# One more block of gates by seven products ahead of attention, and a new distribution of the filling work over the forgetting heads

## The chip, the cores and the metric

The kernel runs on one core of one Trainium2 chip. The core has five engines that run side by side, each through its own list of instructions in order: TensorE (PE) for matrix products, VectorE (DVE), ScalarE (ACT), GpSimd (POOL) and SyncE (SP), which mostly issues DMAs. The metric is the time of one execution on the device, in microseconds (us). Where several executions are given, their median counts.

## The reference, cut to what matters

The layer works on x of 1024 rows by 1024 columns in float32. It is a half feed-forward, then two attentions side by side with gates, then a second half feed-forward and a gated embedding. The middle part is what the change touches:

```python
h = rms_norm(x, mix_norm[i])
fq, fk, fv, f_logit, sq, sk, sv, g_fox, g_sb = split_columns(h @ w_in[i])
fq = rms_norm(fq.reshape(b, s_len, FOX_HEADS, HEAD_DIM), q_norm[i])
fk = rms_norm(fk.reshape(b, s_len, FOX_HEADS, HEAD_DIM), k_norm[i])
log_f = jax.nn.log_sigmoid((f_logit + forget_bias[i]).astype(jnp.float32))
y_fox = forgetting_attention(fq, fk, fv, log_f)
y_sb = stick_breaking_attention(sq, sk, sv)
merged = (jax.nn.sigmoid(g_fox) * (y_fox @ w_branch_fox[i])
          + jax.nn.sigmoid(g_sb) * (y_sb @ w_branch_sb[i]))
x = x + merged @ w_out[i]
```

There are eight forgetting heads (softmax with an added forget term) and eight stick-breaking heads, each 64 wide. The gates g_fox and g_sb are 2048 columns of `h @ w_in`, each passed through a sigmoid. Nothing needs them before the merge, so they may be computed at any time between the norm and the merge.

## The kernel before, in words

Every float32 product is made of three passes over operands that are split into a high part (a rounded copy, by ACT) and a low part (the remainder, by DVE or POOL): high x high, high x low, low x high. A product of 128 gate columns with 512 rows thus takes 3 passes of 8 matmuls, 24 in all, and 48 for all 1024 rows (`g_units`, L915, whose matmuls are at L807).

The gates come in 16 tiles of 128 columns. The first twelve are made ahead of attention by `make_up` (matmuls at L556) in `NG = 6` blocks of 256 columns. A block is a 2 by 2 by 2 product of halves, which `make_up` makes with seven products of 12 matmuls each instead of eight, after sums and differences of the operand blocks have been formed; block 0 alone is made plainly (L506). `up_order` writes out the order of the products, and preparing of weight pieces (`prep`) runs four products ahead. The list `hl` names the buffer for each prepared piece. The order in this stage is the program's.

The last four gate tiles (12 to 15) are made inside attention as filling. `attention` (L1260 on) goes through 16 heads, forgetting heads 0 to 7 and then stick-breaking heads 8 to 15, each in four steps c = 0 to 3 of two blocks of rows. A step emits `scores` of its two row blocks (matmuls at L1050 and L1051) and, two steps late, `apply` (transposes at L1109, copies at L1111 and L1117, value matmuls at L1135). Between these, `take` draws instructions from the head's list in `fill`, at a pace given by the list's total cost, spread over 7, 8, 5 and 6 calls of the four steps (shares 0.27, 0.19, 0.27, 0.27). The first call of a head comes right after the score matmuls of its row block 0, and the last call of a head precedes four value matmuls. The list of a head is used up before the next head begins. All matmuls and transposes go through `pe`, which ties them to the order of emission, so TensorE cannot swap a filling matmul with another one. The order of the other engines inside the forgetting heads is left to a planner that works before the run.

The filling units are:

- `fox_qk_units` (eight units a pair of heads): 24 matmuls of 256 columns each (L799) make q and k of 128 rows. ACT squares and copies them (L863, L864), DVE sums (L865). At t = 3 and t = 7, DVE (L868), POOL with a power (L869) and POOL with a multiplication (L871) norm the half that has just been completed.
- `v_units` (eight units): 24 matmuls of 256 columns each (L799).
- `fox_stack_units` (two halves a head): four transposes of a normed half (L897), then ACT, DVE and four DMAs (L884, L885, L887) put the head's q and k into stacks for the scores. The first half feeds row blocks 0 to 3, the second half row blocks 4 to 7. A half is entered with a cost of 0.436 and a pause of 1.5 that holds no TensorE work.
- `sb_stack_units` and `g_units` (two halves each): 24 matmuls of 512 columns (L807) a half. A gate half ends with a sigmoid on ACT (L926).

Two halves of the filling's weights are split at a time from `RAW` into `WH` (ACT, L129) and `WL` (POOL, L139). There are three buffers of each, so a new cell's weights wait for the buffers of the cell before.

Of the kernel before, what the change touches and what calls it, by code (L numbers as in the profile page):

```python
# [36 lines left out]
def tile_hybrid_decoder_layer(  # L37
# [794 lines left out]
    def v_units(col, extra, cell, new_bank=fill_bank):  # L832
        n = 256 + extra
        add_load(cell, lambda: mix_nat([(col, col + n)], NAT))

        def unit(t):
            weights(cell)
            if t == 0:
                cell["v"] = slot("X", [P, NT, 4, P], F32R)
            ps = new_bank()  # L840
            yield from nat_steps(ps, t, cell["w"], n, hT)
            v2 = cell["v"]
            src = ps[:, :256].rearrange("p (h d) -> p h d", h=4)
            split(v2[:, t, :, 0:HD], v2[:, t, :, HD:P], src, nc.scalar, nc.vector)
            if extra:
                nc.vector.tensor_copy(lfs[:, t, :], ps[:, 256:264])
        return [(24 * 0.109, unit(t)) for t in range(NT)]

    def fox_qk_units(pair, cell, tags=NAT, sq_tag="PT", new_bank=fill_bank):
        add_load(cell, lambda: mix_nat([(FQ + pair * P, FQ + pair * P + P), (FK + pair * P, FK + pair * P + P)], tags))  # L850

        def unit(t):
            weights(cell)
            if t == 0:
                cell["n"] = [slot("RN", [P, 4, 2, 2, HD]) for _ in range(2)]
                cell["ss"] = [stat([P, 4, 4], "qkss", 4) for _ in range(2)]
            half, q = divmod(t, 4)
            ps = new_bank()
            yield from nat_steps(ps, t, cell["w"], 256, hT)
            N = cell["n"][half]  # L860
            src = ps[:, :256].rearrange("p (s h d) -> p s h d", s=2, h=2)
            sq = slot(sq_tag, [P, 256])
            nc.scalar.activation(sq[:].rearrange("p (h s d) -> p s h d", s=2, h=2), src, AF.Square)  # L863
            nc.scalar.copy(N[:, q].rearrange("p h s d -> p s h d"), src)  # L864
            nc.vector.reduce_sum(cell["ss"][half][:, q, :], sq[:].rearrange("p (g d) -> p g d", g=4), axis=AX.X)  # L865
            if q == 3:
                ss = cell["ss"][half][:].rearrange("p a b -> p (a b)")
                nc.vector.tensor_scalar(ss, ss, 1.0 / HD, EPS, ALU.mult, ALU.add)  # L868
                nc.gpsimd.tensor_tensor(ss, ss, mhalf[:], ALU.pow)  # L869
                nv = N[:].rearrange("p a h s d -> p (a h s) d")  # L870
                nc.gpsimd.tensor_mul(nv, nv, ss.unsqueeze(2).broadcast_to([P, 16, HD]))  # L871
        return [(24 * 0.109, unit(t)) for t in range(NT)]
# [44 lines left out]
    def g_units(m, new_bank=fill_bank):  # L917
        cell = {}

        add_load(cell, lambda: wload([kp(win)[:, :, GFOX + m * P:GFOX + m * P + P]], KD, P))  # L920

        def unit(half):
            ps = new_bank()
            yield from feat_steps(ps, half, weights(cell))
            g = slot("PT", [P, 512])
            order("act", nc.scalar.activation(g[:], ps[:], AF.Sigmoid))  # L926
            nc.sync.dma_start(gd[m, :, half * 512:half * 512 + 512], g[:])
        return [(24 * 0.216, unit(0)), (24 * 0.216, unit(1))]
# [250 lines left out]
    FOX_PAIRS = [2, 3, 0, 1]  # L1179
    mx = {}  # L1180

    NG = 6

    def mix_start():

        mx["v"], mx["qk"] = {}, {}
        mx["u1"] = v_units(FV + 256, NH, mx["v"], wide_bank)
        tags = (("T", "Y"), ("T", "Y"))
        mx["u2"] = fox_qk_units(FOX_PAIRS[0], mx["qk"], tags, "KH", wide_bank)
        q0 = FOX_PAIRS[0] * P  # L1190
        pieces = [[kp(win)[:, 4 * kh:4 * kh + 4, a:a + n] for a, n in cols] for cols in (((FV + 256, 256 + NH),), ((FQ + q0, P), (FK + q0, P))) for kh in range(2)]
        raws = {}
        N, Xs = [], []

        def gate_out(n, i, e):
            nc.sync.dma_start(gd[2 * n + i].rearrange("p (h n) -> p h n", h=2), e[:])

        def load_qk(i):
            if i == 0:
                raws["qk"] = [wraw_load(pieces[2 + kh], 4, 256, ("KH", "KL")[kh]) for kh in range(2)]  # L1200
        cycle = ("WL", "WL", "WL", "Q", "Q", "PT")
        hl = ["WL", "WL", "WL", "KL"] + ["PT"] * 4 + ["WL", "WL", "WL", "PT"]
        hl += [cycle[k % 6] for k in range(12, 7 * NG - 6)] + ["WL", "WH", "WH", "Q"]
        tags_g = {"raw": UP_TAGS["raw"], "sum": UP_TAGS["sum"], "w": UP_TAGS["w"], "hl": hl, "t1": "X",
                  "B": {"12": "H", 3: "H", 5: ("Y", "Y", "T", "T"), 6: ("T",) * 4, 7: "X", 4: "X"}}
        F = make_up(N, lambda n: kp(win)[:, :, GFOX + n * 256:GFOX + n * 256 + 256], NG, tags_g, AF.Sigmoid, gate_out, load_qk)
        E = F.E

        def evict(n, m, ps):
            if m == 1:  # L1210
                E[n] = [slot(t, [P, 2, 512]) for t in ("GF", "RN")]
            e1, e2 = E[n]
            if m == 1:
                nc.scalar.copy(e1[:, 0, :], ps[:])
            elif m == 6:
                nc.scalar.copy(e1[:, 1, :], ps[:])
            elif m == 7:
                nc.scalar.copy(e2[:, 1, :], ps[:])
                nc.vector.tensor_add(e2[:, 1, :], e2[:, 1, :], F.bank_of[n, "d"][:])
                nc.scalar.activation(e2[:, 1, :], e2[:, 1, :], AF.Sigmoid)  # L1220
            elif m == 2:
                nc.vector.tensor_add(e1[:, 0, :], e1[:, 0, :], ps[:])
            elif m == 3:
                nc.vector.tensor_add(e1[:, 1, :], e1[:, 1, :], ps[:])
                nc.scalar.activation(e1[:], e1[:], AF.Sigmoid)
                gate_out(n, 0, e1)
            elif m == 4:
                nc.scalar.activation(e2[:, 0, :], ps[:], AF.Sigmoid)
                gate_out(n, 1, e2)
        F.evict = evict  # L1230

        def begin(i, X):
            if not Xs:
                Xs.extend(X)
            up_begin(N, X, mix_norm[0], F, i)

        def end():
            up_first(N, F)
            seqn = up_order(NG)
            L = len(seqn)  # L1240
            for s, (n, m) in enumerate(seqn):
                evict(n, m, F.product(n, m))
                F.begin(s)
                if s + 4 < L:
                    F.prep(*seqn[s + 4])
                if s == L - 16:
                    raws["v"] = [wraw_load(pieces[kh], 4, 256 + NH, "PT") for kh in range(2)]
                elif s == L - 5:
                    mx["v"]["w"] = [wsplit(raws["v"][kh], 4, 256 + NH, ("T", "WL")) for kh in range(2)]
                elif s == L - 2:  # L1250
                    mx["qk"]["w"] = [wsplit(raws["qk"][kh], 4, 256, tags[kh]) for kh in range(2)]
            for cell in loads[:2]:
                cell[1] = None
            B0, B1 = N[0]["B"], (F.B["12"], F.B[3])
            hT.extend([lambda a, k: B0[k // 4][:, a, k % 4, :], lambda a, k: B1[k // 4][:, a, k % 4, :]])
            for _, g in mx["u1"]:
                run(g)
        return types.SimpleNamespace(begin=begin, step=lambda i, t: up_step(N, Xs, xd, F, i, t), end=end)

    def attention():  # L1260
# [8 lines left out]
        def sst(h):  # L1269
            return sb_stack_units(h - 8, stacks[h])  # L1270
# [16 lines left out]
        def any_bank():  # L1287
# [8 lines left out]
        f0 = fst(0, any_bank)  # L1296
        run_all(f0[:1] + p0[1:7] + f0[1:] + p0[7:] + p1)
        qk1, vx = fox_qk_units(fox_pairs[1], qk[1]), v_units(FV, 0, vf0)
        uq2, g12 = fox_qk_units(fox_pairs[2], qk[2]), g_units(12)
        uq3, vy = fox_qk_units(fox_pairs[3], qk[3]), v_units(SV, 0, vs0)  # L1300
        g13, s8, s9 = g_units(13), sst(8), sst(9)
        vz, s10, s11 = v_units(SV + 256, 0, vs1), sst(10), sst(11)
        s12, g14, s13 = sst(12), g_units(14), sst(13)
        s14, g15, s15 = sst(14), g_units(15), sst(15)
        fox_branch = fox_branch_units()
        f = [fst(h) for h in range(1, 8)]
        fill = [mix(f[0], qk1[:7]),
                qk1[7:] + vx[:1] + f[1][:1] + vx[1:4] + f[1][1:],
                mix(f[2], vx[4:] + uq2[:3]),
                uq2[3:] + g12[:1] + f[3][:1] + g12[1:] + f[3][1:],  # L1310
                mix(f[4], uq3[:6]),
                uq3[6:] + vy[:1] + f[5][:1] + vy[1:4] + f[5][1:],
                mix(f[6], vy[4:] + g13[:1]),
                g13[1:] + s8,
                s9 + vz[:2],
                vz[2:5] + s10,
                vz[5:] + s11,
# [357 lines left out]
```

## Time and profile before

| what | value |
|---|---|
| median of three runs | 2271.67 us (2269.41 to 2272.08) |
| profiled execution | 2270.58 us |
| its span, first to last instruction | 2268.9 us |
| PE busy | 2238.0 us (99%) |
| DVE, ACT, POOL busy | 1484.3, 997.9, 801.7 us |
| gate blocks ahead of attention (L556 in one piece) | 689.5 to 779.5 us |
| forgetting heads | 851.9 to 1120.9 us |
| stick-breaking heads | from 1120.9 us |

The span is the time between the first and the last instruction; the execution's own time is 1.7 us longer. A matmul's duration in the trace is longer than the distance to the next one, since matmuls overlap; the cost of a run of matmuls is therefore read from the length of the run. The busy share of PE says little for the same reason, and idle PE time is read from its gaps.

### The profile page before, as it was taken

How to read it: one execution, taken by the hardware profiler on the slowest of the kernel's cores; microseconds unless marked ns; L12 is line 12 of the kernel's file. 1: busy time of each engine (PE TensorE's matmuls, PEld its weight loads, DVE VectorE, ACT ScalarE, POOL GpSimd, SP SyncE). 2: the span in 40 equal slices, each digit the busy share in tenths (PEclk: the TensorE clock that was granted, in tenths of full speed). 3: DMA queues.
4: the chain of work that ended last, by engine and by line, in shares of the span. 5: the costliest groups of instructions: out<-in, count | busy, mean ns of one | idle time of the engine just before them, and what ended most of it. 6: DMA issues, size and time to landing. Idle time of an engine off the chain costs nothing.

```text
span 2268.9 us, 30821 instructions
## 1 busy us (share of the span) xinstructions
PE 2238.0 (99%) x11402; PEld 1902.5 (84%) x11402; DVE 1484.3 (65%) x2303; ACT 997.9 (44%) x1794; POOL 801.7 (35%) x803
## 2 busy tenths in 40 slices
PE   8999999999999999999999999999999999999999
PEld 6888888888888899989798888888888888888888
DVE  8845555688887325666578785789655555778753
ACT  6333333333364435565666663246333333434431
POOL 2444444300011236565566664410544444200121
PEclk9999999999999999999999999999999999999999
DMA  4232323484233333333324366822423232756132
GB/s 140 102 116 88 121 84 125 151 303 172 84 131 125 118 116 99 85 112 85 77 62 95 103 205 220 281 109 64 139 84 125 84 126 83 262 194 220 58 102 84
DMA packets 188936, 291.23 MB, mean 128 GB/s; under 512 B 28393, under 2 KB 104553, under 8 KB 188786
## 3 DMA queue, kind: packets, MB, share of 16 engines
q1 hardware_dynamic: 188784, 289.26, 38.5%
q8 instruction: 90, 1.47, 0.3%
q14 instruction: 60, 0.49, 0.1%
q10 hardware_dynamic: 2, 0.00, 0.0%
HBM read 193.50 MB, written 78.94 MB: 120 GB/s over the span
## 4 chain that ended last, share of the span: by engine, by line
PE 92%; DVE 4%; ACT 2%; issue 1%; DMA 0%; POOL 0%; SPq 0%; ACTq 0%; DVEq 0%; POOLq 0%
PE ps L556 39%; PE ps L454 21%; PE ps L799 7%; PE ps L807 5%; PE ps L1592 4%; PE ps L1397 4%; PE ps L1135 3%; PE ps L506 2%; PE ps L1109 2%; PE ps L1051 1%; PE ps L1050 1%; PE ps L956 1%; PE ps L228 1%; DVE PT L1117 1%; DVE RN L1013 1%
## 5 line engine op out<-in xcount | busy, mean ns | idle before, releaser
L454 PE MATMUL ps<-H,H 128*128 128x512 f32 x2184 | 497.7, 389 | 1.2 <-DVE X L462 1.2
L454 PEld LDWEIGHTS ps<-H,H 128*128 128x128 f32 x2184 | 409.4, 188 | 86.6 <-issue 2.0
L556 PE MATMUL ps<-H,WL 128*128 128x512 f32 x1116 | 264.9, 389 | 0.8 <-ACT WL L105 0.8
L556 PEld LDWEIGHTS ps<-H,WL 128*128 128x128 f32 x1116 | 209.4, 188 | 44.6 <-ACT WL L105 1.2
L556 PE MATMUL ps<-H,Q 128*128 128x512 f32 x612 | 146.0, 389 | 0.0
L462 DVE SCALAR_TENSOR_TENSOR X<-ps,X 128x512 f32<-128x512 f32 x168 | 109.0, 684 | 50.9 <-PE ps L454 50.9
L556 PEld LDWEIGHTS ps<-H,Q 128*128 128x128 f32 x612 | 114.9, 188 | 23.8
L556 PE MATMUL ps<-X,WL 128*128 128x512 f32 x552 | 132.6, 389 | 0.0
L139 POOL TENSOR_TENSOR WL<-RAW,WH 128x512 fp32r<-128x512 f32 (+1 forms) x84 | 98.6, 1196 | 68.0 <-ACT WH L129 42.5
L556 PEld LDWEIGHTS ps<-X,WL 128*128 128x128 f32 x552 | 103.6, 188 | 21.5
L1117 DVE TENSOR_TENSOR PT<-ps,PT 128x512 fp32r<-128x512 f32 (+1 forms) x160 | 100.1, 628 | 31.1 <-ACT PT L1111 30.2
L799 PE MATMUL ps<-WH,H 128*128 128x256 f32 x768 | 116.2, 288 | 1.0 <-ACT RN L864 0.8
L807 PE MATMUL ps<-H,WH 128*128 128x512 f32 x384 | 115.9, 409 | 0.0
L219 POOL TENSOR_SCALAR ss<-ss 128x1 f32<-128x1 f32 x28 | 9.0, 322 | 295.4 <-ACT WL L215 231.9
L1135 PE MATMUL ps<-PT,X 128*128 128x256 f32 (+1 forms) x640 | 102.8, 287 | 8.2 <-DVE PT L1117 5.5
L556 PE MATMUL ps<-H,PT 128*128 128x512 f32 x456 | 108.8, 389 | 0.0
L1111 ACT CAST PT<-ps 128x512 fp32r<-128x512 f32 (+1 forms) x160 | 87.2, 549 | 47.9 <-PE ps L1109 43.9
L1135 PEld LDWEIGHTS ps<-PT,X 128*128 128x128 f32 x640 | 90.7, 191 | 18.6 <-DVE PT L1117 10.2
L799 PEld LDWEIGHTS ps<-WH,H 128*128 128x128 f32 x768 | 101.4, 190 | 3.1 <-ACT RN L864 1.2
L556 PEld LDWEIGHTS ps<-H,PT 128*128 128x128 f32 x456 | 85.5, 188 | 17.7
L1063 POOL TENSOR_TENSOR T<-T,l 128x128 f32<-128x128 f32 (+3 forms) x64 | 73.3, 1149 | 76.0 <-DVE l L1062 75.8
L355 POOL TENSOR_TENSOR PT<-GF,RN 128x512 f32<-128x512 f32 x20 | 33.7, 1687 | 185.4 <-DVE GF L710 185.4
(435 smaller groups left out, 4896.6 us busy)
## 6 DMA issues: line engine op xcount, KB each, us to landing
hidden<-PT SPq DMA_DIRECT2D x40, 512.0 KB, 3.1
WH<-in_ffn_w_gate_dram SPq DMA_DIRECT2D x38, 512.0 KB, 5.5
Q<-hidden SPq DMA_DIRECT2D x24, 512.0 KB, 5.4
hidden<-RN SPq DMA_DIRECT2D x22, 512.0 KB, 2.6
KH<-in_ffn_w_up_dram SPq DMA_DIRECT2D x20, 512.0 KB, 6.3
KL<-in_ffn_w_up_dram SPq DMA_DIRECT2D x20, 512.0 KB, 6.9
T<-in_ffn_w_down_dram SPq DMA_DIRECT2D x20, 512.0 KB, 7.4
X<-in_x_dram SPq DMA_DIRECT2D x16, 512.0 KB, 10.2
```

What stands on the lines that cost most here:

```text
L139: ins = eng_lo.tensor_sub(lo[part], raw[part], f(hi[part]))
L454: pe(nc.tensor.matmul(groups[g][t][:], act[:, a, k, t * P:(t + 1) * P], wt[:, b, k, :], start=(fresh and n == 0), stop=(i in (6, 1, 4) and ...
L462: nc.vector.scalar_tensor_tensor(xs, groups[g][t][:], scale, xs, ALU.mult, ALU.add)
L556: pe(nc.tensor.matmul(ps[:], hl[:, a, k, :], rhs(m, b, k), start=(first and i == 0), stop=(final and i == 11), skip_group_check=True))
L799: pe(nc.tensor.matmul(ps[:, :n], hT[t // 4](a, k)[:, (t % 4) * P:(t % 4 + 1) * P], w[k // 4][b][:, k % 4, :n], start=(i == 0), stop=(i == ...
L807: pe(nc.tensor.matmul(ps[:], w[a][:, k, :], hT[half](b, k), start=(i == 0), stop=(i == 23)))
L1063: nc.gpsimd.tensor_mul(T[:, :n], T[:, :n], l[:].broadcast_to([P, n]))
L1111: high = nc.scalar.copy(pt[:, 0, :width], ps[:, :width])
L1117: ins = nc.vector.tensor_sub(pt[:, 1, :width], ps[:, :width], f(pt[:, 0, :width]))
L1135: pe(nc.tensor.matmul(o, lh, r, start=(kpair == c and i == 0), stop=(kpair == 0 and i == 3)))
L1397: pe(nc.tensor.matmul(ps[:], w[a][:, k, :], yT[g][b][:, k, half * 512:half * 512 + 512], start=(i == 0), stop=(i == 11)))
L1592: pe(nc.tensor.matmul(ps, hT[t // 4](a, k)[:, (t % 4) * P:(t % 4 + 1) * P], pl["w"][d, k // 2][b][:, k % 2, cs], start=(i == 0), stop=(i = ...
```

## The change

`NG` goes from 6 to 7: gate tiles 12 and 13 are made as a seventh block of `make_up` ahead of attention, and their four halves leave the filling of heads 3, 6 and 7. The last entries of `hl` name `KH` and `KL` in place of `WH` for the last prepared pieces, since the seventh block's raw weights now lie in `WH`. The units that are left are dealt anew: heads 0 to 3 get six units of 256 columns each, heads 4 to 6 five each, head 7 one beside the two stack halves of head 8. The second stack half of head 4 (`f[3][1:]`) moves from the end of head 3's list to the start of head 4's own, and that of head 6 (`f[5][1:]`) from the end of head 5's list to the start of head 6's own. Heads 8 to 15 keep their lists.

```diff
-    NG = 6
+    NG = 7
...
-        hl += [cycle[k % 6] for k in range(12, 7 * NG - 6)] + ["WL", "WH", "WH", "Q"]
+        hl += [cycle[k % 6] for k in range(12, 7 * NG - 6)] + ["WL", "KH", "KL", "Q"]
...
-        uq2, g12 = fox_qk_units(fox_pairs[2], qk[2]), g_units(12)
-        uq3, vy = fox_qk_units(fox_pairs[3], qk[3]), v_units(SV, 0, vs0)
-        g13, s8, s9 = g_units(13), sst(8), sst(9)
+        uq2, uq3 = (fox_qk_units(fox_pairs[i], qk[i]) for i in (2, 3))
+        vy, s8, s9 = v_units(SV, 0, vs0), sst(8), sst(9)
...
-        fill = [mix(f[0], qk1[:7]),
-                qk1[7:] + vx[:1] + f[1][:1] + vx[1:4] + f[1][1:],
-                mix(f[2], vx[4:] + uq2[:3]),
-                uq2[3:] + g12[:1] + f[3][:1] + g12[1:] + f[3][1:],
-                mix(f[4], uq3[:6]),
-                uq3[6:] + vy[:1] + f[5][:1] + vy[1:4] + f[5][1:],
-                mix(f[6], vy[4:] + g13[:1]),
-                g13[1:] + s8,
+        fill = [mix(f[0], qk1[:6]),
+                qk1[6:] + vx[:1] + f[1][:1] + vx[1:4] + f[1][1:],
+                mix(f[2], vx[4:] + uq2[:2]),
+                uq2[2:6] + f[3][:1] + uq2[6:],
+                f[3][1:] + f[4][:1] + uq3[:3] + f[4][1:] + uq3[3:5],
+                uq3[5:] + f[5][:1] + vy[:2],
+                f[5][1:] + f[6][:1] + vy[2:5] + f[6][1:] + vy[5:7],
+                vy[7:] + s8,
```

## The prediction

> **What bounds the kernel now.** I read the page first (busy shares and the chain that ended last), then the stages in stretches, then the forgetting heads one by one, then the timeline around the places that the change touches.
>
> ```profile
> span 2268.9 us, 30821 instructions
> PE 2238.0 (99%) x11402; PEld 1902.5 (84%) x11402; DVE 1484.3 (65%) x2303; ACT 997.9 (44%) x1794; POOL 801.7 (35%) x803
> ...
> PE 92%; DVE 4%; ACT 2%; issue 1%; DMA 0%; POOL 0%; SPq 0%; ACTq 0%; DVEq 0%; POOLq 0%
> ```
>
> TensorE bounds the whole: 92% of the chain is its own work. So a matmul taken away is worth its own pitch only where TensorE has no other wait to fall into. The stretches below are the gate blocks, the step between, the forgetting heads and the stick-breaking heads (columns: length, then busy time and count of PE, PEld, DVE, ACT, POOL, then the granted clock, DMA share and GB/s).
>
> ```profile
> 689.50:779.50 90.00, 90.00 (x399) 74.28 (x398) 50.45 (x80) 43.65 (x77) 17.95 (x15) 1.00 0.37 124
> 779.50:851.90 72.40, 72.40 (x520) 67.62 (x519) 19.19 (x60) 28.38 (x56) 28.33 (x22) 1.00 0.40 125
> 851.90:1120.90 269.00, 258.25 (x1907) 243.59 (x1906) 160.56 (x537) 158.80 (x343) 158.50 (x160) 0.99 0.32 89
> 1120.90:1391.00 270.10, 264.08 (x1600) 231.52 (x1599) 212.54 (x355) 165.78 (x366) 169.35 (x257) 1.00 0.45 128
> ```
>
> The gate blocks have no idle TensorE at all, and the other engines are far from full there (DVE 50.45 of 90). The forgetting heads are different: TensorE idles 269.00 - 258.25 = 10.75 us. Head by head, from head 0 to head 7:
>
> ```profile
> 851.90:881.50 29.60, 28.48 (x224) 27.26 (x223) 15.18 (x60) 14.89 (x37) 18.12 (x16) 1.00 0.40 124
> 881.50:911.80 30.30, 29.07 (x231) 27.98 (x230) 19.43 (x66) 17.45 (x40) 20.38 (x21) 1.00 0.23 63
> 911.80:946.70 34.90, 34.29 (x278) 33.58 (x277) 22.77 (x73) 20.96 (x47) 19.46 (x21) 1.00 0.47 129
> 946.70:986.60 39.90, 39.73 (x279) 36.66 (x278) 21.36 (x69) 24.48 (x50) 26.06 (x24) 1.00 0.21 60
> 986.60:1021.00 34.40, 31.63 (x255) 30.73 (x254) 22.21 (x71) 21.17 (x49) 18.18 (x18) 1.00 0.40 116
> 1021.00:1053.60 32.60, 31.78 (x255) 30.82 (x254) 20.61 (x70) 19.37 (x44) 24.80 (x26) 1.00 0.27 66
> 1053.60:1086.20 32.60, 31.46 (x231) 29.46 (x230) 21.40 (x69) 18.86 (x41) 17.62 (x21) 1.00 0.41 113
> 1086.20:1120.90 34.70, 31.81 (x174) 27.11 (x173) 17.60 (x61) 21.61 (x40) 13.90 (x17) 0.95 0.19 47
> ```
>
> Idle TensorE is 1.12, 1.23, 0.61, 0.17, 2.77, 0.82, 1.14 and 2.89 us. Head 3, with the most filling, hardly idles; heads 4 and 7 idle most, and head 7 alone has a clock below full.
>
> **The change, part by part.** First the work of TensorE, from the chain in order of time (start, length, what):
>
> ```profile
> 689.54 89.99 PE ps L556 x396
> 779.53 46.23 PE ps L799 x384
> ...
> 973.03 2.77 PE ps L807 x12
> ...
> 1110.07 2.76 PE ps L807 x12
> ```
>
> A matmul of the gate blocks has a pitch of 89.99 / 396 = 0.227 us, one of a gate tile in the filling 2.76 / 12 = 0.230 us, one of 256 columns 46.23 / 384 = 0.120 us. The seventh block adds seven products of 12 matmuls: 84 x 0.227 = +19.1 us, all on the path, since that stage has no idle TensorE. Four gate halves leave: 96 x 0.230 = -22.1 us. Together **-3.0 us**. The block's splits and sums on the other engines cost nothing: the stage's DVE is busy 56%, ACT 49%, POOL 20%, and one block more keeps the ratio. Its two weight loads and two gate stores carry the bytes that the gate tiles' loads and stores carried later. The new buffer names cost nothing either: the last pieces take `KH` and `KL` buffers whose raw weights were split at least two products (2 x 12 x 0.227 = 5.4 us) before. The low part of one v weight now waits for the fourth-last product, and four products (4 x 12 x 0.227 = 10.9 us) cover it. The 72.40 us stretch behind the block is full of TensorE work and stays as it is. Moving whole 256-column units between heads 0 and 7 changes no count.
>
> Second, ACT. A sigmoid among exponentials makes ACT load a table twice:
>
> ```profile
> 979.80 1.28 ACT L1061 ACT_TABLE_LOAD   x1
> ...
> 985.46 1.28 ACT L926 ACT_TABLE_LOAD   x1
> ...
> 986.57 0.22 PE L1050 MATMUL ps<-KH,Q 128*128 128x128 f32 x1
> 986.63 0.28 PE L1051 MATMUL ps<-KL,Q 128*128 128x128 f32 x1
> ...
> 987.40 0.66 PE L897 MATMUL ps<-identf,RN 128*128 128x128 f32 x4 [0.50 <-ACT PT L926]
> ...
> 988.34 1.28 ACT L1061 ACT_TABLE_LOAD   x1
> ...
> 992.75 0.63 PE L1109 MATMUL ps<-identf,T 128*128 128x128 f32 x4 [2.04 <-DVE l L1062]
> ...
> 1091.29 0.63 PE L1109 MATMUL ps<-identf,T 128*128 128x128 f32 x4 [0.91 <-DVE l L1062]
> ...
> 1099.88 1.28 ACT L1061 ACT_TABLE_LOAD   x1
> ...
> 1102.51 0.39 PE L1135 MATMUL ps<-PT,X 128*128 128x256 f32 x1 [1.64 <-ACT PT L1111]
> ```
>
> With the four gate halves go the sigmoids and the loads around them. The idle stretches of TensorE that end right behind such loads are 0.50 + 2.04 + 0.91 + 1.64 = 5.1 us. The exponential or the copy that they wait for is then early, and what is late next is the next copy in the same chain, usually by some tenths. The bounds are 0 (another wait takes the place) and -5.1; I take **-4.0**, since heads 1 and 5 with like filling idle 1.23 and 0.82 where heads 4 and 7 idle 2.77 and 2.89, a difference of about 1.8 a head, to which the shorter waits below the trace's threshold add a little.
>
> Third, the moved stack half of head 4. Its transposes read q and k of rows 512 to 1023 in normed form, and the last of these is unit t = 7 of `uq2`. In the old list two gate halves, and with them over 11 us of matmuls, stood between that unit and the transposes. In the new one `uq2[7]` is the last of head 3's list and the transposes are the first of head 4's. Between them TensorE has four value matmuls (4 x 0.120) and the two score matmuls at 986.57 and 986.63, some 0.65 us. What has to happen meanwhile is shown by the same unit in the old kernel:
>
> ```profile
> 967.87 5.04 POOL L139 TENSOR_TENSOR WL<-RAW,WH 128x512 fp32r<-128x512 f32 x4 [1.94 <-ACT WH L129]
> ...
> 968.58 0.64 PE L799 MATMUL ps<-WL,H 128*128 128x256 f32 x4
> ...
> 969.26 0.38 ACT L863 ACTIVATE PT<-ps 128x256 f32<-128x256 f32 x1
> ...
> 969.84 0.41 DVE L865 TENSOR_REDUCE qkss<-PT 128x4 f32<-128x256 f32 x1
> ...
> 973.30 2.91 POOL L869 TENSOR_TENSOR qkss<-qkss,mhalf 128x16 f32<-128x16 f32 x1
> ...
> 976.29 1.91 POOL L871 TENSOR_TENSOR RN<-RN,qkss 128x1024 f32<-128x1024 f32 x1
> ```
>
> From the end of the last matmul at 969.22 to the end of the multiplication at 978.20 are 9.0 us. Without any queue the durations alone sum to 0.38 + 0.41 + 2.91 + 1.91 = 5.6 us; with POOL's low weight parts ahead (5.04 us) it is 9.0; and at a head's end the 1.9 us scaling of the last row block may queue too. So TensorE waits 5.6 - 0.65 = 5 to 10 us there, and every matmul of head 4 is queued behind the transposes. Only one cell's half of weights comes free at that place (2.5 us of POOL instead of 5.04), so I take 8 us from matmul to norm, rounded up for the row scaling, and a wait of **+7.4**. While it lasts the other engines catch up, which I put at **-0.8**, the ordinary idle time of a head. The other moved half, head 6's, has `f[5][:1]` and two v units (48 x 0.120 = 5.8 us of matmuls, more with what lies between) behind `uq3[7]` and costs nothing; if that cover were gone it would cost the same 5 to 10. That the second half now arrives within its own head:
>
> ```profile
> 985.22 0.60 PE L897 MATMUL ps<-identf,RN 128*128 128x128 f32 x4
> ...
> 996.19 0.55 SPq L887 DMA_DIRECT2D KL<-KL  x1
> ...
> 1005.55 0.31 PE L1050 MATMUL ps<-KH,Q 128*128 128x320 f32 x1
> ```
>
> From these transposes to the issue of the half's last DMA are 11.0 us, and row block 4 comes 1005.55 - 986.57 = 19.0 us into the head, of which the thinner list takes some 4. The transposes and the row block are shifted by the same wait, so 19.0 - 4 - 0.7 - 11.0 = some 3 us are left for that DMA to land, and I cost it at 0 (up to +3 if the DMAs queue).
>
> Fourth, the clock. Head 7 shows what a gap does (stretches of 3.4 us):
>
> ```profile
> 1100.50:1103.90 3.40, 1.42 (x9) 1.01 (x8) 1.45 (x3) 2.44 (x5) 2.04 (x4) 0.99 0.67 164
> 1103.90:1107.30 3.40, 3.40 (x13) 3.04 (x12) 0.41 (x1) 0.37 (x1) 0.00 (x0) 0.50 0.33 72
> ```
>
> A stretch with TensorE busy 1.42 of 3.40 us is followed by one at half clock, which loses 1.7 us. That event hangs on the 1.64 us wait behind the table loads and should go (-1.7). A wait of 7 us should bring one in head 4 (+1.7; bounds 0 and 3.4, two stretches). Net **0**. [...]
>
> Fifth, thinner cover. TensorE work between dependent steps shrinks in heads 0, 2, 3, 4, 5 and 7 and grows in head 1. Head 3 would idle like heads 1 or 2 (+0.4 to +1.1), heads 5 and 7 by a few tenths more. I take **+1.5**, with bounds 0 (nothing waits that did not) and +5 (every thinned head idles another 0.8, as between heads 3 and 1).
>
> Sum: -3.0 - 4.0 + 7.4 - 0.8 + 0 + 1.5 = **+1.1 us** on the profiled 2270.58, or 2271.7. The median of the runs is 1.1 above the profiled run, so the forecast is **2272.8 us**. About 0.2% (4.5 us) is what a measurement of this kernel can tell from no change.
>
> **The rivals.** *The wait at head 4 decides (slower).* POOL has all of its four low weight parts and the row scaling ahead of the power: 9.0 + 1.9 - 0.65 = 10.2 us instead of 7.4, a second half-clock stretch (+1.7), and table loads that give only 2 us since other waits follow (+2.0): +1.1 + 2.8 + 1.7 + 2.0 = +7.6, so 2279. It decides from a wait of some 11 us on, all else equal, or from 9 us with half of the other gain lost. For it speaks that the row at 967.87 stands ahead of the power; against it that one cell less comes free there.
>
> *The wait is short (faster).* The planner puts the power first: 5.0 us, no half clock in head 4 (-1.7), the full 5.1 of the table waits, no thinner cover: -3.0 - 5.1 + 5.0 - 0.8 - 1.7 = -5.6, so 2266. For it speaks that POOL is busy only 14 to 26 us of a head; against it that both splits and row scaling come due just then.
>
> *The filling was not on the path.* If the forgetting heads were bound by their chain of ACT, DVE and POOL, the four gate halves would have been free and the block would cost its whole 19.1 us: 2271.7 + 19.1 = 2291. The heads' lengths speak against it: head 3, with the gate tile, is 39.90 long at 39.73 busy.
>
> **How the numbers follow.** The forecast, within 0.2% of the old time, has 0.42; the slow rival 0.36; the fast one 0.20; the last 0.02. The wait's bounds alone (5 to 10) with the bounds of the table waits and the cover give 2265 to 2282 when the extremes don't all meet, and I take 2265 to 2282 as the range. The forecast's own range is 2268 to 2277. Faster 0.20, same 0.42, slower 0.38.
>
> **What would show it.** One piece of L556 19 us longer ahead of attention, without gaps. No table load in the forgetting heads. At the first transposes (L897) of head 4 an idle TensorE of 5 to 10 us, released by POOL's L871, and a stretch at half clock behind it; none in head 7. No like wait in head 6. Heads 0 to 7 together 269.0 + 1.1 - 19.1 = 251 us. Wrong would be the prediction if that wait is absent or under 4 us, if another place idles by more than 3 us, or if the seventh block is not 19 us long.

## The result, and the profile after

The changed kernel takes 2277.64 us (median of 8 runs, 2275.43 to 2278.56) against 2270.18 us before (8 runs, 2269.41 to 2272.08): a ratio of 1.003, 95% interval 1.002 to 1.004. It is 7.5 us slower. The profiled execution took 2277.1 us, 6.5 more than the one before.

The page of the changed kernel, its busy line and its chain:

```profile
span 2275.3 us, 30813 instructions
PE 2236.0 (98%) x11390; PEld 1903.1 (84%) x11390; DVE 1492.5 (66%) x2313; ACT 991.6 (44%) x1793; POOL 801.3 (35%) x803
...
PE 92%; DVE 5%; ACT 2%; issue 1%; POOL 1%; DMA 0%; DVEq 0%; ACTq 0%; POOLq 0%
```

TensorE is busy 2 us less and the span is 6.4 us longer, and POOL's share of the chain goes from 0% to 1%. The chain in order of time shows the gate blocks in one piece, and POOL's weight parts at the start of head 4:

```profile
689.14 109.03 PE ps L556 x480
...
994.06 1.35 POOL WL L139 x2
995.41 1.09 issue
996.51 2.93 POOL WL L139 x2
```

The piece is 109.03 - 89.99 = 19.0 us longer for 84 matmuls more, and has no gap. (`issue` is time for which the profile shows nothing that was waited for.) The forgetting heads 0 to 7 follow in stretches (columns as in the prediction), then all eight together, then two short stretches in head 4 and two in head 6, each time the wait and the time behind it:

```profile
870.50:896.70 26.20, 25.54 (x200) 24.59 (x199) 14.78 (x59) 14.35 (x35) 17.64 (x16) 1.00 0.46 138
896.70:929.30 32.60, 31.79 (x255) 30.83 (x253) 20.23 (x69) 19.24 (x43) 22.23 (x23) 1.00 0.24 66
929.30:961.80 32.50, 31.40 (x254) 30.58 (x253) 21.52 (x70) 19.59 (x43) 17.31 (x21) 1.00 0.45 125
961.80:993.40 31.60, 30.96 (x250) 30.34 (x249) 20.13 (x68) 18.56 (x45) 17.69 (x19) 1.00 0.13 40
993.40:1035.70 42.30, 31.35 (x235) 30.37 (x234) 22.98 (x72) 19.70 (x48) 23.98 (x23) 0.88 0.38 100
1035.70:1064.60 28.90, 28.20 (x226) 27.34 (x225) 19.69 (x67) 18.32 (x43) 21.24 (x21) 1.00 0.27 62
1064.60:1099.40 34.80, 30.66 (x235) 29.64 (x234) 21.99 (x70) 18.11 (x41) 18.73 (x21) 0.95 0.31 87
1099.40:1126.80 27.40, 27.12 (x174) 24.25 (x173) 18.01 (x63) 17.43 (x37) 14.92 (x19) 1.00 0.25 58
870.50:1126.80 256.30, 237.02 (x1811) 227.95 (x1810) 159.32 (x537) 145.32 (x329) 153.75 (x156) 0.97 0.31 85
...
993.70:1004.30 10.60, 0.05 (x1) 0.00 (x0) 2.84 (x7) 2.19 (x7) 10.52 (x8) 0.74 0.43 124
1004.30:1008.90 4.60, 4.56 (x22) 4.29 (x22) 1.87 (x7) 1.91 (x4) 0.34 (x1) 0.50 0.17 41
1066.97:1070.38 3.41, 0.36 (x4) 0.12 (x2) 2.28 (x8) 2.22 (x6) 3.41 (x4) 1.00 0.41 154
1070.38:1073.79 3.41, 3.06 (x15) 3.09 (x16) 2.49 (x7) 1.59 (x4) 1.90 (x5) 0.50 0.66 151
```

The forgetting heads are 12.7 us shorter than before (256.3 against 269.0), and the prediction wanted 18 us. Heads 4 and 6 hold the difference: TensorE idles 10.95 and 4.14 us in them, under 1.2 in each of the others, and only these two have a clock below full (0.88 and 0.95). No table load is left in them. The timeline around the two places:

```profile
991.97 1.12 PE L799 MATMUL ps<-WL,H 128*128 128x256 f32 x8
992.21 1.89 POOL L1063 TENSOR_TENSOR T<-T,l 128x1024 f32<-128x1024 f32 x1 [0.41 <-DVE l L1062]
...
994.06 5.37 POOL L139 TENSOR_TENSOR WL<-RAW,WH 128x512 fp32r<-128x512 f32 x4
...
999.40 2.90 POOL L869 TENSOR_TENSOR qkss<-qkss,mhalf 128x16 f32<-128x16 f32 x1
...
1002.38 1.90 POOL L871 TENSOR_TENSOR RN<-RN,qkss 128x1024 f32<-128x1024 f32 x1
...
1004.34 1.12 PE L897 MATMUL ps<-identf,RN 128*128 128x128 f32 x4 [10.59 <-POOL RN L871]
1052.36 5.03 POOL L139 TENSOR_TENSOR WL<-RAW,WH 128x512 fp32r<-128x512 f32 x4 [1.99 <-ACT WH L129]
...
1062.39 1.90 POOL L871 TENSOR_TENSOR RN<-RN,qkss 128x1024 f32<-128x1024 f32 x1
...
1064.25 3.10 POOL L1063 TENSOR_TENSOR T<-T,l 128x768 f32<-128x768 f32 x2
...
1067.32 0.86 POOL L1042 TENSOR_TENSOR T<-GF,mask_fox 128x128 f32<-128x128 f32 x2
1067.80 0.29 DVE L1055 CUSTOM_DVE_ANT_0 T<-T,ps 128x128 f32<-128x128 f32 x1 [2.17 <-POOL T L1042]
...
1068.13 0.40 ACT L1061 ACTIVATE T<-T,m 128x128 f32<-128x128 f32 x1 [1.85 <-DVE m L1055]
...
1070.73 1.09 PE L1109 MATMUL ps<-identf,T 128*128 128x128 f32 x4 [3.41 <-DVE PT L1117]
```

Head 4 begins as the prediction said: the last q and k unit ends at 993.09, four value matmuls and two score matmuls follow, and then TensorE stands for 10.59 us before the moved half's transposes, until POOL has scaled the last row block (1.89), made four low weight parts (5.37), and normed (2.90 + 1.90). Head 6 is another case. Its moved half starts without a wait worth the name, but the norm and the weight parts have pushed POOL's row scalings and mask additions (L1063, L1042) so far back that DVE waits 2.17 us for the first mask, ACT waits for DVE, the copies that free a bank of the transposes wait behind ACT's exponential, and TensorE stands for 3.41 us.

### The profile page after: what moved, and what is told of

The parts are those of the page before. It is cut to its first block, busy times and chain, and to the rows that moved or that the text cites. A ratio compares the mean times of both kernels' runs of the same rounds, so it can differ in the third digit from the quotient of the medians.

```text
span 2275.3 us, 30813 instructions
## 1 busy us (share of the span) xinstructions
PE 2236.0 (98%) x11390; PEld 1903.1 (84%) x11390; DVE 1492.5 (66%) x2313; ACT 991.6 (44%) x1793; POOL 801.3 (35%) x803
## 4 chain that ended last, share of the span: by engine, by line
PE 92%; DVE 5%; ACT 2%; issue 1%; POOL 1%; DMA 0%; DVEq 0%; ACTq 0%; POOLq 0%
PE ps L556 40%; PE ps L454 21%; PE ps L799 7%; PE ps L1591 4%; PE ps L807 4%; PE ps L1396 4%; PE ps L1135 3%; PE ps L506 2%; PE ps L1109 2%; PE ps L1051 1%; PE ps L1050 1%; PE ps L956 1%; DVE PT L1117 1%; PE ps L228 1%; DVE RN L1013 1%
## 5 line engine op out<-in xcount | busy, mean ns | idle before, releaser
L556 PE MATMUL ps<-H,Q 128*128 128x512 f32 x636 | 151.8, 389 | 0.0
L556 PE MATMUL ps<-X,WL 128*128 128x512 f32 x588 | 141.2, 389 | 0.0
L556 PEld LDWEIGHTS ps<-X,WL 128*128 128x128 f32 x588 | 110.4, 188 | 22.9
L1117 DVE TENSOR_TENSOR PT<-ps,PT 128x512 fp32r<-128x512 f32 (+1 forms) x160 | 100.0, 627 | 26.7 <-ACT PT L1111 25.3
L139 POOL TENSOR_TENSOR WL<-RAW,WH 128x512 fp32r<-128x512 f32 (+1 forms) x80 | 92.7, 1181 | 59.8 <-ACT WH L129 36.3
L1135 PEld LDWEIGHTS ps<-PT,X 128*128 128x128 f32 x640 | 90.9, 192 | 14.9 <-DVE PT L1117 9.0
L1063 POOL TENSOR_TENSOR T<-T,l 128x128 f32<-128x128 f32 (+3 forms) x64 | 73.6, 1154 | 68.1 <-DVE l L1062 68.0
L807 PE MATMUL ps<-H,WH 128*128 128x512 f32 x320 | 97.0, 407 | 0.0
```

The lines of the kernel that those rows point to most:

```text
L139: ins = eng_lo.tensor_sub(lo[part], raw[part], f(hi[part]))
L556: pe(nc.tensor.matmul(ps[:], hl[:, a, k, :], rhs(m, b, k), start=(first and i == 0), stop=(final and i == 11), skip_group_check=True))
L807: pe(nc.tensor.matmul(ps[:], w[a][:, k, :], hT[half](b, k), start=(i == 0), stop=(i == 23)))
L1063: nc.gpsimd.tensor_mul(T[:, :n], T[:, :n], l[:].broadcast_to([P, n]))
L1117: ins = nc.vector.tensor_sub(pt[:, 1, :width], ps[:, :width], f(pt[:, 0, :width]))
L1135: pe(nc.tensor.matmul(o, lh, r, start=(kpair == c and i == 0), stop=(kpair == 0 and i == 3)))
```

## The experiments

All times are compared with runs of the kernel before on the same chip (2270.6 and 2270.8 us); ratios are to these. Where the changed kernel's 2277.64 us was measured, the kernel before took 2270.18, so a difference from the changed kernel is uncertain by some 0.6 us.

### The wait in head 4, taken away

```diff
...
-            N = cell["n"][half]
+            N = cell["n"][rows[half]]
...
+        f[3] = fox_stack_units(qk[2], 0, stacks[4], rows=(0, 0))
```

> The changed kernel, but the second stack half of head 4 is filled from the normed q and k of rows 0 to 511 instead of rows 512 to 1023, which have long been normed: head 4's rows 512 to 1023 come out with other values, the work stays the same. Theory (one wait at the first transposes of head 4, 10.6 us long, and the half clock behind it): the idle stretch at L897 goes, the half clock behind it (some 2.3 us lost) too, and up to 3 us come back as another wait, since POOL's queue is as full as before: 10 to 13 us less than the changed kernel, about 2266. Rival (the gate tiles' cover is missing everywhere in the forgetting heads): at most 4 us less, the idle time appears at other places of heads 3 to 5.

Measured: 2268.44 us, ratio 0.9992 (0.9983 to 1.0001), 9.2 us less than the changed kernel. Head 4 in the changed kernel without the wait (its stretch):

```profile
993.70:1027.00 33.30, 29.68 (x234) 28.30 (x233) 21.83 (x72) 19.34 (x47) 23.89 (x23) 1.00 0.47 127
```

It is 33.3 long instead of 42.3, with the clock at full. All that is gained lies in this one head; the others keep their lengths, head 6 with its wait of 3.41 us too. So one wait and its half clock, and not a lack of cover everywhere, cost 9 us net. Two waits of 1.8 and 1.3 us for DVE's copies (L1117) took a part of its place, which is why the gain is just under the 10 to 13 expected.

### The half moved alone, in the old kernel

The first try put the gate tile ahead of the last units but also brought head 4's first half late.

```diff
-                uq2[3:] + g12[:1] + f[3][:1] + g12[1:] + f[3][1:],
-                mix(f[4], uq3[:6]),
+                uq2[3:5] + g12 + uq2[5:7] + f[3][:1] + uq2[7:],
+                f[3][1:] + mix(f[4], uq3[:6]),
```

> The kernel before with its six gate blocks and all gate tiles in the filling; only head 3's list is dealt so that the gate tile comes ahead of the last q and k units, and the second stack half of head 4 comes first in head 4. Theory: TensorE waits 9 to 11 us for the norm at the start of head 4, with half clock behind it: 2279 to 2284, that is 9 to 14 us over the kernel before. Rival (the loss needs the thinner lists): within 3 us of the kernel before.

Measured: 2281.05 us, ratio 1.0046 (1.0034 to 1.0059). The time is as expected, but the reason is not the one that was to be tested. TensorE's idle stretches at the start of head 4:

```profile
988.60 0.33 PE L1050 MATMUL ps<-KH,Q 128*128 128x128 f32 x1 [2.37 <-DMA KH<-KH]
...
994.31 0.47 PE L1051 MATMUL ps<-KL,Q 128*128 128x128 f32 x1 [5.39 <-DMA KL<-KL]
...
997.62 1.11 PE L897 MATMUL ps<-identf,RN 128*128 128x128 f32 x4 [2.83 <-POOL RN L871]
```

Most of the wait, 7.8 us, is for the DMAs of the first half, which this list brought too late. The run can't tell the theories apart, so it was made again with the first half early:

```diff
-                uq2[3:] + g12[:1] + f[3][:1] + g12[1:] + f[3][1:],
-                mix(f[4], uq3[:6]),
+                uq2[3:4] + g12 + f[3][:1] + uq2[4:],
+                f[3][1:] + mix(f[4], uq3[:6]),
```

> The kernel before with its six gate blocks and both gate tiles; in head 3's list the gate tile and head 4's first stack half stand ahead of the last four q and k units, and head 4's second stack half comes first in head 4. So the first half is early and only the second one follows its norm at once. Theory: one wait of 7 to 11 us at the first transposes of head 4, released by POOL's multiplication, with two or three stretches of half clock: 2278 to 2284. Rival (with the gate tile still in the list nothing is lost): within 3 us of the kernel before.

Measured: 2282.45 us, ratio 1.005 (1.0037 to 1.0062), 11.6 us over the kernel before. POOL and TensorE in the timeline there:

```profile
987.79 5.40 POOL L139 TENSOR_TENSOR WL<-RAW,WH 128x512 fp32r<-128x512 f32 x4 [0.44 <-ACT WH L129]
993.16 2.90 POOL L869 TENSOR_TENSOR qkss<-qkss,mhalf 128x16 f32<-128x16 f32 x1
996.14 1.90 POOL L871 TENSOR_TENSOR RN<-RN,qkss 128x1024 f32<-128x1024 f32 x1
...
998.10 1.11 PE L897 MATMUL ps<-identf,RN 128*128 128x128 f32 x4 [9.37 <-POOL RN L871]
```

The time and the wait are as expected. It is the same wait, 9.37 us, now in a kernel with six gate blocks and all its gate tiles in the filling, one of them only earlier in head 3's list. Order alone makes it: a stack half right behind the norm that it reads. The seventh block has no part in it other than that it takes away the matmuls that stood between.

### The table loads by themselves

```diff
-            order("act", nc.scalar.activation(g[:], ps[:], AF.Sigmoid))
+            order("act", nc.scalar.activation(g[:], ps[:], AF.Copy if m < 14 else AF.Sigmoid))
```

> The kernel before, but gate tiles 12 and 13 are copied without their sigmoid (those gates come out without it), so that ACT loads no table in the forgetting heads; TensorE's instructions are the same. Theory (the table loads cost what the prediction took, 4.0 us, and hold up head 7's clock): 3 to 6 us less than the kernel before, about 2265.5, and no half clock in head 7. Rival (another wait takes their place): within 1.5 us of the kernel before.

Measured: 2263.48 us, ratio 0.9969 (0.9958 to 0.998), 7.1 us less than the kernel before with TensorE's instructions unchanged. Heads 4 and 7 there:

```profile
987.20:1019.60 32.40, 31.20 (x255) 30.62 (x253) 22.05 (x72) 18.67 (x46) 17.62 (x18) 1.00 0.42 123
1084.70:1114.50 29.80, 29.80 (x174) 25.83 (x173) 17.52 (x61) 16.55 (x36) 13.87 (x17) 1.00 0.21 54
```

They are 2.0 and 4.9 us shorter than before, and head 7's clock is at full; no table load stands in the forgetting heads. Eight loads of 1.28 us on ACT, an engine busy 44%, cost TensorE 7 us. They stand in ACT's queue ahead of copies and exponentials that TensorE waits for (in the prediction's rows the wait of 1.64 us for a copy follows such a load), and 1.7 us of the 7 are the half clock of head 7. The gain is a little above the range expected, and it needs no seventh block.

### Whose queue it is: weight parts on DVE

```diff
...
+        uq2, uq3 = fox_qk_units(fox_pairs[2], qk[2]), fox_qk_units(fox_pairs[3], qk[3], low=nc.vector)
+        vy, s8, s9 = v_units(SV, 0, vs0, low=nc.vector), sst(8), sst(9)
```

> The changed kernel, but the low parts of the weights of the fourth q and k cell and of the v cell behind it are made by DVE instead of POOL. Theory (POOL's four weight parts, 5.4 us, stand ahead of the norm's power in the waits of heads 4 and 6): the wait at head 4 shrinks from 10.6 to 5 or 6 us, the one in head 6 from 3.4 to under 1 us, together 6 to 9 us less than the changed kernel, about 2270. Rival (the norm's own 4.8 us on POOL and the row scaling set the wait): under 3 us less. DVE's own additions of some 0.7 us each may take a part back.

Measured: 2273.4 us, ratio 1.0013 (1.0004 to 1.0022), 4.2 us less than the changed kernel. The waits:

```profile
1002.79 1.12 PE L897 MATMUL ps<-identf,RN 128*128 128x128 f32 x4 [8.11 <-POOL RN L871]
...
1067.53 0.92 PE L1109 MATMUL ps<-identf,T 128*128 128x128 f32 x4 [1.94 <-DVE PT L1117]
```

Both shrink, and by less than expected: 10.59 to 8.11, and 3.41 to 1.94. The gain lies between the theory's 6 to 9 and the rival's 3. In head 4 the parts now stand in DVE's queue ahead of the norm's sum (three of them, 2.95 us, against 5.37 on POOL), and the difference, 2.4 us, is what the first wait lost. So work queued ahead on POOL sets a part of both waits. Of the 10.59 us the trace gives 5.37 to the weight parts and 4.80 to the norm's own two operations on POOL.

### Head 6's half moved back

```diff
-                uq3[5:] + f[5][:1] + vy[:2],
-                f[5][1:] + f[6][:1] + vy[2:5] + f[6][1:] + vy[5:7],
+                uq3[5:] + f[5][:1] + vy[:2] + f[5][1:],
+                mix(f[6], vy[2:7]),
```

> The changed kernel with the second stack half of head 6 back at the end of head 5's list, all else as changed. Theory (the 3.4 us wait in head 6 comes from POOL's queue: four weight parts and the norm, 10 us of work, put the row scalings and the mask additions of head 6's first rows behind): the wait stays at 2 to 4 us and the time within 1.5 us of the changed kernel. Rival (the half's own copies on ACT and DVE at the start of head 6 make it): the wait and the half clock behind it go, 3 to 5 us less than the changed kernel.

Measured: 2276.13 us, ratio 1.0024 (1.0014 to 1.0033), 1.5 us less than the changed kernel. The stretches after the start of head 6:

```profile
1066.30:1069.70 3.40, 1.51 (x11) 1.33 (x11) 2.74 (x7) 2.44 (x6) 3.19 (x5) 1.00 0.34 78
1069.70:1073.10 3.40, 2.54 (x13) 2.54 (x13) 2.59 (x9) 1.21 (x4) 0.88 (x2) 0.50 0.92 253
1073.10:1076.50 3.40, 3.40 (x18) 3.40 (x17) 0.05 (x1) 0.00 (x0) 0.61 (x1) 0.50 0.45 129
```

The idle time is still there (now in two pieces of 1.73 and 1.05 us) and the half clock lasts twice as long. Head 6 is 35.1 us long against 34.8. What DVE and TensorE wait for:

```profile
1066.90 0.29 DVE L1055 CUSTOM_DVE_ANT_0 T<-T,ps 128x128 f32<-128x128 f32 x1 [1.90 <-POOL T L1042]
...
1068.01 0.36 PE L799 MATMUL ps<-WH,H 128*128 128x256 f32 x1 [1.73 <-DVE KL L885]
```

DVE again stands for POOL's first mask, 1.90 us against 2.17, and TensorE then waits for a stack half's copy that stood behind it in DVE's queue. So the moved half is not needed for the loss. One stack half, the first of head 7, still comes first in head 6's list; but the kernel before starts head 6 with the same half, and idles only 1.14 us in the whole head.

### Two other deals without gate tiles

The old lists with the gate halves struck out:

```diff
...
+        fill = [mix(f[0], qk1[:7]),
+                qk1[7:] + vx[:1] + f[1][:1] + vx[1:4] + f[1][1:],
+                mix(f[2], vx[4:] + uq2[:3]),
+                uq2[3:] + f[3],
+                mix(f[4], uq3[:6]),
+                uq3[6:] + vy[:1] + f[5][:1] + vy[1:4] + f[5][1:],
+                mix(f[6], vy[4:]),
+                s8,
```

> Seven gate blocks as in the changed kernel, but the lists of the forgetting heads are those of the kernel before with the gate halves struck out: no half moves into its own head. Theory: with the gate tile gone the norm of the last q and k unit of head 3 is still waited for, but behind that unit lie a stack half's pause and head 3's own last steps: a wait of 4 to 8 us at the end of head 3 instead of 10.6, head 6's wait gone since that norm falls into the middle of head 5: 2264 to 2270. Rival (the moved halves alone make the loss, not the lost cover): no wait there at all, about 2260.

Measured: 2274.87 us, ratio 1.0019 (1.001 to 1.0028), where 2264 to 2270 was expected. TensorE's waits, and what POOL and DVE do ahead of the second:

```profile
1000.60 1.12 PE L897 MATMUL ps<-identf,RN 128*128 128x128 f32 x4 [7.40 <-POOL RN L871]
1010.56 1.12 PE L1109 MATMUL ps<-identf,T 128*128 128x128 f32 x4 [4.17 <-DVE PT L1117]
```

```profile
1005.37 1.89 POOL L1063 TENSOR_TENSOR T<-T,l 128x1024 f32<-128x1024 f32 x1 [2.36 <-DVE l L1062]
1005.63 2.17 DVE L1171 TENSOR_TENSOR Y<-Y,PT 128x512 fp32r<-128x512 f32 x1 [0.34 <-ACT PT L1170]
```

The wait for the norm is there without any moved half, 7.40 us as expected, and one of 4.17 us behind it in head 4, which was not. The second is no wait for the norm: a subtraction on DVE (L1171) took 2.17 us, where the same instruction took 0.71 us in head 6 of the changed kernel (POOL was scaling a row block beside both), and ACT's exponential, with the copies behind it, waited for DVE. No run tests why it took so long. Head 6's wait is down to 1.5 us: it has four units in place of five, and the norm now falls into the middle of head 5. Heads 6 and 7 are 26.9 and 24.5 us long on their thin lists, the shortest of all.

The second deal gives head 3 four units, all its norms done early by the list's costs, and a longer pause:

```diff
+        f[3] = fox_stack_units(qk[2], 0, stacks[4], pause=4.0)
...
+                qk1[7:] + vx[:1] + f[1][:1] + vx[1:5] + f[1][1:],
+                mix(f[2], vx[5:] + uq2[:4]),
+                uq2[4:] + f[3],
...
```

> Seven gate blocks, no gate halves, and lists dealt so that both norms fall into the middle of a head: heads 0 to 7 get 7, 6, 7, 4, 6, 5, 5 and 0 units, no half moves into its own head, and the stack halves of head 4 take a longer pause each, so that they come late in head 3. Theory (the change's gain is real: 3.0 us of matmuls and the table loads of some 7 us, lost only to the two waits): no wait over 1.5 us in heads 3 to 6, 2258 to 2262, faster than both kernels. Rival (thin lists bring waits of their own: head 3 has four units, head 7 none but two stack halves): 2266 and over.

Measured: 2277.82 us, ratio 1.0035 (1.0023 to 1.0048). The theory expected 2258 to 2262 and was wrong here:

```profile
1000.26 0.47 PE L897 MATMUL ps<-identf,RN 128*128 128x128 f32 x1 [7.78 <-POOL RN L871]
...
1013.04 1.09 PE L1109 MATMUL ps<-identf,T 128*128 128x128 f32 x4 [3.62 <-DVE l L1062]
```

The time lies in the rival's range (2266 and over), but the longer wait stands at the same place as in the deal before, and the one of 3.62 us comes at the same transposes as the 4.17 us there. A pause is a cost in the list, not work. `take` draws nothing in it, TensorE has only the head's own steps, and the wait of 7.78 us is no shorter than the 7.40 before. Head 3 also has a unit less here, so the pause by itself was not tried.

### A version with real work behind the norm

The units put behind `uq2` in head 3 here are v units, whose weights would have to stay in buffers that `uq2` needs. So the last four v units load their weights a second time.

```diff
...
+        qk1, vx = fox_qk_units(fox_pairs[1], qk[1]), v_units(FV, 0, vf0, split_at=4)
+        uq2 = fox_qk_units(fox_pairs[2], qk[2])
+        later[0]()
+        uq3 = fox_qk_units(fox_pairs[3], qk[3])
...
+                mix(f[2], uq2[:6]),
+                uq2[6:] + f[3][:1] + vx[4:7] + f[3][1:] + vx[7:],
+                mix(f[4], uq3[:6]),
+                uq3[6:] + vy[:1] + f[5][:1] + vy[1:4] + f[5][1:],
+                mix(f[6], vy[4:]),
+                s8,
```

> Seven gate blocks and no gate halves in the forgetting heads, but the last four v units of the first half of the heads are made from a second load of their weights, so that they can stand behind the last q and k unit of head 3: three of them (72 matmuls of 0.120 us) come between the last norm and the stack half of head 4 that needs it; no half moves into its own head. Theory (only matmuls behind the norm cover it; an entry's pause doesn't): no wait over 1.5 us at that place and no half clock there, 2258 to 2263, 7 to 12 us under the kernel before. Rival (the forgetting heads without gate tiles have too little work, so a wait comes wherever the units stand): 2268 and over. The second load costs POOL 5 us and ACT 2 us, which should lie beside TensorE's work.

Measured: 2266.43 us, ratio 0.9983 (0.9974 to 0.9992): 4.4 us under the kernel before and 11.2 under the changed one. The forgetting heads together and TensorE's longest wait in heads 3 and 4 (L1116 and L1069 of this kernel are L1109 and L1062 of the others):

```profile
871.10:1116.20 245.10, 233.89 (x1812) 224.17 (x1811) 158.23 (x536) 145.05 (x330) 158.04 (x159) 1.00 0.34 93
```

```profile
1003.88 0.63 PE L1116 MATMUL ps<-identf,T 128*128 128x128 f32 x4 [1.84 <-DVE l L1069]
```

No wait for the norm is left and the clock is full throughout; 72 matmuls behind the norm cover it. The time stays above the 2258 to 2263 expected. Waits of 1.2 to 1.8 us remain in heads 1, 2, 3, 4 and 6; what each of these is worth was not measured. The lists of all eight heads changed at once, so the run shows what the whole deal is worth and not each place.

## Why the prediction was right or wrong

The time lies in the range of 2265 to 2282, but the likeliest case (2268 to 2277) did not come: 7.5 us slower where about 1 to 2 was forecast. Of the prediction's own signs of being wrong one came: another place, in head 6, idles by more than 3 us. The slow rival (2279, by a wait of 10.2 us at the same place) came closest, and its number in part by luck: its wait and its second stretch of half clock came, its weak table loads (2 us) did not, and head 6, at which it had nothing, made up for them. By the steps of the prediction, as changes of the profiled lengths:

| step | forecast | measured |
|---|---|---|
| matmuls: block in, gate halves out | -3.0 | +19.0 - 22.1 = -3.1 |
| table loads, with head 7's half clock | -4.0 - 1.7 | -6.9 (heads 4 and 7 of the run without sigmoid) |
| head 4: wait, half clock, catching up | +7.4 + 1.7 - 0.8 = +8.3 | +12.3 |
| head 6's moved half | 0 | +4.3 |
| thinner cover elsewhere | +1.5 | about -0.6 |
| sum | +1.1 | +6.0 of the 6.4 us that the span grew |

Head 4's entry is its length, 42.3, less what it would be: 34.4 before, less one unit (24 x 0.120 = 2.9), less 2.0 for the table loads, plus 0.5 for four transposes more, which is 30.0. Of the 12.3 the wait is 10.6 and the half clock 2.3 (4.6 us of work at half), and 0.6 comes back. Head 6's: 34.8 less 32.6 + 2.9 - 5.5 + 0.5 = 30.5. The cover: heads 0, 1, 2, 3 and 5 are 167.3 - 151.8 = 15.5 us shorter, and the matmuls that they lost (one unit in all, two gate halves, eight transposes) come to 14.9. Against the forecast, heads 4 and 6 err by 8.3 us one way and the other steps by 3.4 the other; that the time stayed in the range is in part this offset, and so luck.

- The first step held, the block and the gaps alike.
- In the second the mechanism was right and the size too small, 5.7 for 6.9 (7.1 by the medians). I took less than the visible stretches because another wait should take their place; the run shows that little did.
- The third step named the place, the releaser and the half clock, and failed in one term: "Only one cell's half of weights comes free at that place (2.5 us of POOL instead of 5.04)". POOL made four parts there, 5.37 us, since both halves of the fourth cell's weights came due at the end of `uq2`. That is 2.9 of the 3.2 us by which the wait was longer. The row at 967.87 had shown four parts, and the slow rival counted them. The upper bound of 10 us was itself 0.6 short.
- "The other moved half, head 6's, ... costs nothing" was wrong for the head, though right for the half: it starts at once. The price came from POOL's queue at the end of head 5, which the prediction did not look at. The run with the half moved back keeps the loss; the run with the weight parts on DVE nearly halves the wait.
- The second stack half was in time in its own head, as costed: no score matmul of row block 4 waits for a DMA.
- The fourth step set head 4's half clock off against head 7's. Head 7's did go, as it does in the run without sigmoid, where only the table loads are missing: it hung on the wait behind them, as the prediction had read from its row. But two came: 2.3 us in head 4, and 1.5 in head 6 (3.06 us of work at half).
- The fifth step was too dear: heads 2 and 3 idle 0.5 us more each, as foreseen for head 3, but heads 0, 1 and 5 together 1.0 less. It also left out head 6, whose list gets thinner too (a v unit of 2.9 us in, a gate half of 5.5 us out).
- The last rival's 2291 is a slip: with the gate halves free, their 22.1 us would have to be taken back from the forecast, which gives 2295. The measured time is far from both.

What the change gains, some 10 us of matmuls and table loads, is thus real, and it loses more than that by two waits. The first needs neither the seventh block (it comes with six) nor the moved half (7.40 us without it), only a norm with too few matmuls behind it; taking the gate tiles out of the lists left it so. With three v units behind the norm it is gone.

## What to carry to other kernels

When filling work is taken out of a list, look at what it stood between: a producer whose chain runs over other engines (here 2.90 and 1.90 us on POOL, behind 5.37 us of weight parts) needs matmuls behind it before TensorE's queue comes to the consumer. With next to none the wait was 9.37 and 10.59 us, with the 72 matmuls of three v units behind it there was none for the norm, and a pause in a planner's list, which is not such work, left one of 7.78 us. Read the length of such a chain with the queue that really stands ahead of it (weight parts, scalings), not from its own instructions, and ask the same of the work that queues behind it. Ask also what a function costs on the path that makes ACT load its table: here eight loads of 1.28 us, on an engine busy 44%, cost 7.1 us.

## What the runs showed of the hardware

In the changed kernel the granted clock was 0.50 from 1070.38 to 1073.79, 3.41 us with the wait of 3.41 us in head 6, and from 998.70 to 1008.94, 10.24 us or three times as much with the wait of 10.59 us in head 4. The wait alone did not set it: in the deal with the longer pause the clock was 0.50 for the same 10.24 us with a wait of 7.78 us, and for 6.83 us with one of 3.62 us:

```profile
994.62:1004.86 10.24, 4.60 (x18) 4.11 (x19) 3.15 (x11) 1.74 (x5) 7.35 (x6) 0.50 0.56 120
1011.65:1018.48 6.83, 5.44 (x26) 5.47 (x27) 2.60 (x7) 1.19 (x3) 1.83 (x4) 0.50 0.50 134
```

In both long waits the half clock started while TensorE still stood: at 998.70 in a wait that ended at 1004.34, and at 994.62 in one that ended at 1000.26. So 4.6 us of each 10.24 lie behind the wait. In the changed kernel four transposes (L897) took 1.12 us in them, against 0.62 us at full clock at the start of head 6, and half of the 4.6, 2.3 us, is counted as lost above. Four transposes behind the wait of 7.40 us in the old deal without gate tiles took 1.12 us too.

Shorter waits went both ways. In the run with head 6's half moved back, the stretch with TensorE busy 1.51 of 3.40 us, whose longest wait was 1.73 us, was followed by two stretches at a clock of 0.50. The single waits of 2.04 us in head 4 of the kernel before and of 1.84 us in the run with three v units behind the norm were followed by none: the clock is 1.00 in that head's row and in that run's.
